# Opening of a hybrid encoder block re-ordered, and the w_up products kept in PSUM for the convolution

## The chip, the cores and the metric

The kernel runs on one core of a Trainium2 chip. A core has TensorE (matrix products, with weight loads that overlap them), VectorE, ScalarE, GpSimd, and SyncE, whose queue (SP) issues most of the DMAs; SBUF is the working memory, PSUM the eight banks into which TensorE writes. The metric is the device time of one execution in microseconds (us).

## The reference

One layer of a bidirectional encoder: 1024 positions, 1024 features, float32. A conditioning vector c gives six vectors of 1024 (shift, scale and gate, twice). The block is two token mixers in parallel, then a feed-forward network with a convolution over positions:

```python
ada = jax.nn.silu(c) @ w_ada[i] + b_ada[i]
shift1, scale1, gate1, shift2, scale2, gate2 = jnp.split(ada, 6, axis=-1)
h = rmsnorm(x, g_mix[i]) * (1 + scale1) + shift1
qa, ka, va, qb, kb, vb, ga, gb = jnp.split(h @ w_in[i], split_at, axis=-1)
oa = mixture_of_dilations(qa, ka, va, rel_bias)           # 8 heads of 64
ob = neighbourhood_attention_2d(qb, kb, vb, na_rpb[i])    # 8 heads of 64
merged = sigmoid(ga) * (oa @ w_branch_dil[i]) + sigmoid(gb) * (ob @ w_branch_na[i])
x = x + gate1 * (merged @ w_out[i])
h2 = rmsnorm(x, g_ffn[i]) * (1 + scale2) + shift2
u = depthwise_conv_seq(h2 @ w_up[i], conv_w[i], conv_b[i])   # width 3, centred
u_val, u_gate = jnp.split(u, 2, axis=-1)                     # 2816 each
x = x + gate2 * ((gelu(u_gate) * u_val) @ w_down[i])
return rmsnorm(x, g_final)
```

w_ada has 6144 columns, w_in 5120, w_up 5632.

## The kernel before

Features lie on the 128 partitions, positions on the free axis in two halves of 512. x comes transposed, as eight tiles of 128 features. Every large product is done in three passes: each operand is split into a rounded high part and a low remainder, and high x high, high x low and low x high are summed in PSUM. So every operand needs a ScalarE copy (the high part, `whi`, `h`, lines 57 and 207) and a subtraction on VectorE or GpSimd (the low part, lines 61 and 209).

**Opening** (from line 384, its order on all engines written out by hand). SP loads x's first half, then w_ada's first quarter, parts of w_in's q, k and v columns, further quarters of w_ada, and x's second half. In the meantime TensorE multiplies the identity with itself (`warm`, line 215), a product that nothing reads. ScalarE squares x (line 185), VectorE adds the squares in two groups of four, TensorE sums them over features with one-column products against ones (`add_sums`, line 98). `rstd_of` gives the root mean square, `bcast` spreads it by four transposes into a PSUM bank (`pb`). Of `ada`'s first 2048 values (shift1, scale1) only a quarter is needed at a time: a quarter is eight rows of w_ada, times c. VectorE sums six rows (`ada_rows`), TensorE takes the other two and that sum by one-column products (`ada_sums`, line 153).

Then come four pieces, q = 0 to 3. Each finishes a quarter of `ada` (`piece_bias`, lines 274 and 276), makes two feature tiles of h (`modulate`: VectorE multiplies x by scale and `pb`, ScalarE adds the shift and rounds, VectorE takes the low part), and lets TensorE add these two tiles into two 512-column products (q and k of the first heads, `qk_products`, lines 84 to 86) and into four groups of 256 columns (v, lines 246 to 248). Between these stand the next quarter's rows and sums. Afterwards come the other v half, the statistics of x's second half (`square_sums`, `bcast`), the writing out of q and k, and h's second half.

**Middle.** Attention heads, then the branch products, the gates and w_out. There x is read a second time from HBM.

**w_up** (from about 840 us). It has 22 blocks; each is a two by two block product done with seven products of combined operands instead of eight. `STEPS` names them: 11 x B11, S2 x T2, S1 x T1, S3 x T3, 12 x B21, S4 x B22, 22 x T4, each of 12 matmuls of 512 columns, into four PSUM banks a, b, c and d (`pj`, a ring of six). `products` (line 1191) adds the banks together on VectorE: line 1217 after the second step, 1219 after the third, 1222 after the fourth, 1230 after the sixth, 1234 after the seventh. `a_operands` prepares the weights (GpSimd lines 1159 to 1161 and 61, ScalarE line 57). The results go to the convolution: `conv_in` (line 1425) on ScalarE for the middle tap, `conv_taps` (line 1431) on VectorE for the other two, in six pieces. For the first three blocks the convolution waits until both halves of a row block are there. In the two remaining banks lie the statistics (`pcol`, `pbc`), and later the staging copies for w_down (`moved`).

Outside the hand-ordered parts a planner orders each engine's instructions when the program is built: it runs through them with estimated durations and takes by priority what its estimates find ready. It also gives out the buffers. So another cost or place in one part can move instructions in a later one.

Of the kernel before, what the change touches and what calls it, by code (L numbers as in the profile page):

```python
# [29 lines left out]
def hybrid_encoder(tc, xT, c, w_ada, small, w_in, p1_bias, p23_bias, na_bias, ln2_mult, ident, w_br, w_out,  # L30
# [83 lines left out]
    def h_tile(dtype=FR):  # L114
# [8 lines left out]
    homes = iter([(qkpool, "kl", 4)] + [(qkpool, n, b) for n, b in (("qs", 4), ("ks", 4), ("qb", 2))  # L123
                                        for _ in range((3, 3, 1)[("qs", "ks", "qb").index(n)])]
                 + [(early, "wada", 3)] * 2 + [(adapool, "wada", 4)] * 4 + [(qkpool, "qb", 2), (early, "wada", 3)])
# [19 lines left out]

    def ada_sums(parts, pa=None, stop=True, n=4, new=None):
# [15 lines left out]
    def ada_rows(wt, ts, acc=None):  # L162

        for t in ts:
            if acc is None:
                acc = wt[t]
                dve.tensor_scalar(acc, acc, cs[:, t:t + 1], None, OP.mult)
            else:
                dve.scalar_tensor_tensor(acc, wt[t], cs[:, t:t + 1], acc, OP.mult, OP.add)

    def x_load(hf, ks=range(KT)):
        x = []
        for k in ks:
            x.append(h_tile(FT))
            sp.dma_start(x[-1], xT[k][:, halves[hf]])
        return x
# [22 lines left out]
    def modulate(x, hf, ks, pb):  # L199

        last = ()
        for k in [*ks, None]:
# [7 lines left out]
            last = k is not None and (lo, t, b, f(hi))  # L210

# [57 lines left out]
    act.activation(sig, cs, AF.Sigmoid)  # L269
    dve.tensor_tensor(cs, cs, sig, OP.mult)  # L270
# [113 lines left out]
    with tc.manual_schedule(engines={e.engine for e in (sp, act, dve, pool, pe)}):  # L384
# [11 lines left out]
        wt.append(ada_load(3))  # L396
        x.append(x_load(1))
        qk_w = [[wpool.tile([128, KT, 128], FR, name=n) for n in ("whi", "wlo")] for _ in range(2)]
# [3 lines left out]
        first = ps_s.tile([128, 512], FT, name="pv", bufs=3)  # L402
        stage = [None, first]
# [12 lines left out]
        warm(12, first[:, :128], True)  # L416
        stage[0] = ps_n.tile([128, 512], FT, name="pcol")
        qk_split(0, (pool, pool))
        v_split(v_raw, (pool, pool), slice(0, 4), v_w[0])
        pvs = [v_banks()]  # L420
        for q in range(4):
            ks = range(2 * q, 2 * q + 2)
            if q == 2:
                v_raw1 = v_load(0, 1)
            piece_bias(q, pa)
            modulate(x[0], 0, ks, pb)
            qk_products(ks)
            if q < 3:
                ada_rows(wt[q + 1], range(6))
            if q == 0:  # L430
                qk_split(1, (dve, dve))
                v_split(v_raw, (dve, dve), slice(4, 8), v_w[0])
            if q == 2:
                v_split(v_raw1, (dve, dve), slice(0, KT), v_w[1])
            if q == 3:
                accs = sq_accs()
                square(x[1], accs, range(8), dve)
            v_products(0, (0, 1), ks)
            if q < 3:
                pa = ada_sums([(wt[q + 1][t], cs[:, t:t + 1]) for t in (6, 7)], stop=False)  # L440
                ada_sums([(wt[q + 1][0], ones)], pa)
# [1334 lines left out]
```

## Time and profile before

| | us |
|---|---|
| median of 3 runs | 1524.02 (1523.12 to 1525.61) |
| the profiled execution | 1522.23 |
| its span in the profile | 1520.5 |
| TensorE busy in the span | 1484.7 |
| mean granted TensorE clock | 0.991 |

A group's row in the profile reads: line, engine, operation, what is written from what, form, count, then busy us and mean ns, then the idle time before and what ended it. A timeline row reads: start, duration, engine, line, operation, operands. A row of waits: engine and line, what it waited for, total us, times, longest. A row of windows: start and end, length, then for PE, PEld (weight loads), DVE (VectorE), ACT (ScalarE) and POOL (GpSimd) busy us and count; then the granted clock, the busy share of the DMA engines, and GB/s. Matmuls are pipelined, so the duration of one (0.39 us) is longer than the distance to the next (0.23 us), and PE can count as busy though it waited for a moment.

### The profile page before, as it was taken

The page shows a single profiled execution, that of the slowest core. Times are in us where ns is not written, and L with a number is a line of the kernel's source. Part 1 is how long each engine was busy: PE and PEld are TensorE (multiplying, and loading weights), DVE is VectorE, ACT ScalarE, POOL GpSimd, SP SyncE. Part 2 cuts the span into 40 slices and gives each one's busy share as a digit, 9 for nine tenths or more (in the row PEclk, how much of TensorE's full clock was granted, in tenths as well). Part 3 has the DMA queues.
Part 4 walks back from the last instruction along what each step waited for, and adds up shares of the span by engine and source line. Part 5 has one row for each costly group of instructions (what it writes and reads, how often), then busy time and mean ns, then how long its engine had stood idle before and what let it go on. Part 6 is the DMA issues. An engine that isn't in the chain of part 4 may idle for free.

```text
span 1520.5 us, 21650 instructions
## 1 busy us (share of the span) xinstructions
PE 1484.7 (98%) x7680; PEld 1263.0 (83%) x7680; DVE 964.0 (63%) x1768; ACT 770.2 (51%) x1439; POOL 751.7 (49%) x624
## 2 busy tenths in 40 slices
PE   8999999999999999999999989999999998999997
PEld 8888888889798998878888868888888887878787
DVE  5775345465545655645515898766666668787765
ACT  4331566665655666643346553444444447575542
POOL 1021343424234454522268588776666665778721
PEclk9999999999999999999999999999999999999999
DMA  9567332434645555577644122222222224513323
GB/s 354 191 239 258 100 109 75 147 87 136 182 134 151 143 159 164 171 253 234 199 155 139 70 84 83 101 101 84 83 82 83 83 78 153 199 58 130 113 56 111
DMA packets 117299, 210.27 MB, mean 138 GB/s; under 512 B 42788, under 2 KB 55716, under 8 KB 117156
## 3 DMA queue, kind: packets, MB, share of 16 engines
q1 hardware_dynamic: 116920, 208.64, 42.6%
q8 instruction: 60, 0.98, 0.3%
q14 instruction: 47, 0.39, 0.1%
q10 hardware_dynamic: 272, 0.26, 0.1%
HBM read 163.58 MB, written 42.66 MB: 136 GB/s over the span
## 4 chain that ended last, share of the span: by engine, by line
PE 77%; DMA 6%; DVE 6%; POOL 5%; ACT 3%; issue 2%; SPq 0%; DVEq 0%; POOLq 0%; ACTq 0%
PE pj L84 10%; PE pj L86 10%; PE pj L85 10%; PE pj L1209 10%; PE pj L1210 10%; PE pj L1211 10%; PE pj L367 3%; PE O L937 2%; DMA wraw<-w_down 1%; POOL wsl L61 1%; DVE big L1431 1%; PE T L924 1%; PE S L902 1%; DMA fb<-fcs 1%; PE O L768 1%
## 5 line engine op out<-in xcount | busy, mean ns | idle before, releaser
L61 POOL TENSOR_TENSOR wlo<-wraw,whi 128x512 fp32r<-128x512 f32 (+1 forms) x94 | 116.1, 1257 | 172.0 <-ACT whi L57 138.0
L84 PE MATMUL pj<-h,whi 128*128 128x512 f32 x448 | 184.7, 412 | 2.2 <-ACT h L207 2.2
L85 PE MATMUL pj<-h,whi 128*128 128x512 f32 x448 | 176.1, 393 | 2.1 <-DVE h L209 2.1
L86 PE MATMUL pj<-h,wlo 128*128 128x512 f32 x448 | 175.9, 393 | 0.0
L61 POOL TENSOR_TENSOR wsl<-big,wsh 128x512 fp32r<-128x512 f32 (+1 forms) x86 | 116.7, 1379 | 45.0 <-ACT wsh L57 44.2
L641 POOL TENSOR_TENSOR wlo<-wraw,whi 128x512 fp32r<-128x512 f32 x58 | 75.1, 1306 | 116.2 <-ACT whi L640 103.5
L591 DVE TENSOR_TENSOR tl<-T,th 128x512 fp32r<-128x512 f32 (+3 forms) x120 | 77.2, 654 | 87.2 <-ACT th L590 85.8
L583 ACT ACTIVATE P<-P,st 128x256 f32<-128x256 f32 x128 | 64.2, 502 | 94.3 <-DVE st L582 94.3
L1431 DVE SCALAR_TENSOR_TENSOR big<-wc,sm,big 128x256 f32<-128x256 f32 (+1 forms) x129 | 100.8, 826 | 15.1 <-ACT big L1425 15.1
L86 PEld LDWEIGHTS pj<-h,wlo 128*128 128x128 f32 x448 | 84.1, 188 | 18.5
L85 PEld LDWEIGHTS pj<-h,whi 128*128 128x128 f32 x448 | 84.7, 189 | 13.9 <-DVE h L209 3.4
L84 PEld LDWEIGHTS pj<-h,whi 128*128 128x128 f32 x448 | 84.5, 189 | 14.1 <-ACT h L207 2.8
L57 ACT ACTIVATE whi<-wraw 128x1024 fp32r<-128x1024 f32 (+2 forms) x51 | 49.4, 971 | 70.8 <-PE pj L85 26.0
L915 POOL TENSOR_SCALAR P<-P,stb 128x288 f32<-128x288 f32 (+1 forms) x32 | 40.1, 1254 | 88.3 <-DVE stb L912 72.7
L61 POOL TENSOR_TENSOR wsl<-wraw,wsh 128x384 fp32r<-128x384 f32 (+1 forms) x46 | 53.6, 1186 | 57.8 <-ACT wsh L57 57.7
L1431 DVE SCALAR_TENSOR_TENSOR big<-pj,sm,big 128x512 f32<-128x512 f32 (+1 forms) x129 | 66.4, 563 | 15.7 <-ACT big L1425 15.7
L590 ACT ACTIVATE th<-T 128x512 fp32r<-128x512 f32 (+3 forms) x120 | 65.5, 565 | 20.4 <-PE T L924 13.0
L57 ACT ACTIVATE wsh<-big 128x1024 fp32r<-128x1024 f32 (+1 forms) x43 | 42.9, 997 | 51.8 <-POOL big L1160 37.0
L549 POOL TENSOR_TENSOR vv<-vv 128x512 fp32r<-128x512 f32 (+1 forms) x40 | 41.9, 1066 | 47.0 <-ACT vv L548 45.8
L582 DVE CUSTOM_DVE_ANT_0 P<-S,bias 128x256 f32<-128x256 f32 x128 | 48.8, 419 | 22.2 <-POOL bias L679 11.5
L908 ACT ACTIVATE P<-P,stb 128x288 f32<-128x288 f32 (+1 forms) x64 | 36.4, 569 | 47.6 <-DVE stb L906 47.6
L1457 ACT ACTIVATE big<-big 128x1024 f32<-128x1024 f32 x22 | 23.3, 1061 | 65.3 <-DVE big L1431 65.3
(426 smaller groups left out, 4744.0 us busy)
## 6 DMA issues: line engine op xcount, KB each, us to landing
wraw<-w_in SPq DMA_DIRECT2D x34, 512.0 KB
wada<-w_ada SPq DMA_DIRECT2D x31, 512.0 KB
big<-w_up SPq DMA_DIRECT2D x22, 512.0 KB
wraw<-w_up SPq DMA_DIRECT2D x22, 512.0 KB
as<-big SPq DMA_DIRECT2D x22, 512.0 KB
big<-as SPq DMA_DIRECT2D x22, 512.0 KB
wraw<-w_down SPq DMA_DIRECT2D x24, 384.0 KB
gs<-gs SPq DMA_DIRECT2D x32, 256.0 KB
```

What stands on the lines that cost most here:

```text
L57: act.activation(hi, raw, AF.Copy)
L61: lo_eng.tensor_tensor(lo[:, i:i + step], raw[:, i:i + step], f(hi)[:, i:i + step], OP.subtract)
L84: pe.matmul(psum, whi[:, k0 + k], mhi, start=k == 0, stop=False)
L85: pe.matmul(psum, whi[:, k0 + k], mlo, start=False, stop=False)
L86: pe.matmul(psum, wlo[:, k0 + k], mhi, start=False, stop=k == n - 1)
L590: act.activation(th[:m, :n], pt[:m, :n], AF.Copy)
L591: dve.tensor_tensor(tl[:m, :n], pt[:m, :n], f(th)[:m, :n], OP.subtract)
L641: pool.tensor_tensor(lo[:, i:i + n], raw[:, i:i + n], f(hi)[:, i:i + n], OP.subtract)
L1209: pe.matmul(psum, whi[:, k], bhi, start=j < 4 and k == 0, stop=False, skip_group_check=True)
L1210: pe.matmul(psum, whi[:, k], blo, start=False, stop=False, skip_group_check=True)
L1211: pe.matmul(psum, wlo[:, k], bhi, start=False, stop=k == n - 1, skip_group_check=True)
L1431: dve.scalar_tensor_tensor(y[:, dst], src, wt, y[:, dst], OP.mult, OP.add)
```

## The change

In the opening: c and the identity are loaded by ScalarE's queue. x's layout in HBM is changed, and its first half comes in four DMAs of two tiles each. TensorE sums the last two squared tiles itself. It takes w_ada's rows 0 and 1 directly; VectorE's sum of rows lies in a PSUM bank. Of the identity passes 9 + 2 + 2 + 2 + 2 + 5 are left, standing between the sums. x is multiplied by `pb` ahead of the pieces (four tiles by VectorE, four by GpSimd from a copy), and `scaled` then makes the high part in one ScalarE pass and, in a second pass, the float32 value from which VectorE takes the low part. The products of a tile ask for the low part last. Rows of w_ada are summed ahead, seven by VectorE and one by TensorE in two of the quarters. GpSimd takes more low parts. The last quarter of w_ada goes to other buffers, and w_in's second v half is loaded early. Among the v groups behind the pieces, the sums and the broadcast of x's second half are moved.

In w_up: for all blocks but the last, the result of the fourth step is written to a PSUM bank of the tags `pcol` and `pbc` in turn, and that of the seventh stays in its own bank.

```diff
-    sp.dma_start(idt, ident)
-    sp.dma_start(cs, c)
+    act.dma_start(cs, c)
+    act.dma_start(idt, ident)
...
+    def ada_rows_load(j):
+        rows = [h_tile(FT) for _ in range(KT)]
+        for t, w in enumerate(rows):
+            sp.dma_start(w, w_ada[j][:, t])
+        return rows
...
+    def ada_rows(wt, acc, ts, first, last):
         for t in ts:
+            col, dst = cs[:, t:t + 1], wt[t] if t == last else acc
+            if t == first:
+                dve.tensor_scalar(dst, wt[t], col, None, OP.mult)
             else:
+                dve.scalar_tensor_tensor(dst, wt[t], col, acc, OP.mult, OP.add)
...
+    def scaled(x, k):
+        hi, lo = h[0, k] = h_tile(), h_tile()
+        t, b, g = stage[k % 2], ada[:, k:k + 1], am1[:, k:k + 1]
+        act.activation(hi, x, AF.Identity, bias=b, scale=g)
+        act.activation(t, x, AF.Identity, bias=b, scale=g)
+        return lambda: dve.tensor_tensor(lo, t, f(hi), OP.subtract)
...
     def qk_products(ks):
         for k in ks:
-            for p, w in zip(qk_psum, qk_w):
-                product(p, w, lambda k: h[0, k], ks=[k])
+            mhi, mlo = h[0, k]
+            for x_, (part, m) in enumerate(((0, mhi), (1, mhi), (0, mlo))):
+                for p, w in zip(qk_psum, qk_w):
+                    pe.matmul(p, w[part][:, k], m, start=k + x_ == 0, stop=k == KT - 1 and x_ == 2)
...
-        warm(28, first[:, :128], True)
+        warm(9, idle, True)
         accs = sq_accs()
-        square(x[0], accs, range(8), dve)
-        pcol = square_sums(accs, lambda: warm(8, first[:, :128], True))
-        ada_rows(wt[0], range(3))
+        square(x[0], accs, range(6), dve)
+        last = [early.tile([128, 512], FT, name="mt", bufs=3) for _ in range(2)]
+        for sq, xk in zip(last, x[0][6:]):
+            act.activation(sq, xk, AF.Square)
+        pcol = ps_n.tile([128, KT], FT, name="pcol")
+        for i, sq in enumerate(accs + last):
+            add_sums(pcol, sq, i == 0, i == 3)
+            if i == 0:
+                warm(2, idle, True)
+            if i == 1:
+                warm(2, idle, True)
+            if i == 2:
+                pa = ada_sums([(wt[0][0], cs[:, 0:1])], stop=False)
+                warm(2, idle, True)
+        ada_rows(wt[0], acc, range(2, 6), 2, 7)
         rs = rstd_of(pcol, 4)
-        warm(4, first[:, :128], True)
+        qk_split(0, (pool, pool))
+        ada_sums([(wt[0][1], cs[:, 1:2])], pa, stop=False)
         pb = bcast(rs, ps_n, "pbc")
-        ada_rows(wt[0], range(3, 6), wt[0][0])
-        pa = ada_sums([(wt[0][t], cs[:, t:t + 1]) for t in (6, 7)], stop=False)
-        ada_sums([(wt[0][0], ones)], pa)
-        warm(12, first[:, :128], True)
+        pbs = early.tile([128, 512], FT, name="mt", bufs=3)
+        act.activation(pbs, pb, AF.Copy)
+        ada_rows(wt[0], acc, range(6, 8), 2, 7)
+        for k in range(2):
+            dve.tensor_tensor(x[0][k], x[0][k], pb, OP.mult)
+        warm(2, idle, True)
+        ada_sums([(wt[0][7], ones)], pa)
+        warm(5, idle, True)
         for q in range(4):
             ks = range(2 * q, 2 * q + 2)
             piece_bias(q, pa)
-            modulate(x[0], 0, ks, pb)
+            if q == 0:
+                for k in range(2, 4):
+                    dve.tensor_tensor(x[0][k], x[0][k], pb, OP.mult)
+                stage = [ps_n.tile([128, 512], FT, name=n) for n in ("pcol", "pbc")]
+            low = [scaled(x[0][k], k) for k in ks]
+            if q == 0:
+                v_split(v_raw, (pool, pool), slice(0, 4), v_w[0])
+                for k in range(4, 8):
+                    pool.tensor_tensor(x[0][k], x[0][k], pbs, OP.mult)
+            if q == 1:
+                qk_split(1, (pool, pool))
+                v_split(v_raw, (pool, pool), slice(4, 8), v_w[0])
...
+            if q == 0:
+                pa = ada_sums([(wt[1][t], cs[:, t:t + 1]) for t in (6, 7)], stop=False)
+                v_parts(0, range(4), ks, (0,))
+                ada_sums([(wt[1][5], ones)], pa)
+                v_parts(0, range(4), ks, (1, 2))
+                continue
...
-        pcol = square_sums(accs)
-        v_products(1, (1,), range(8))
-        pb = bcast(rstd_of(pcol, 4), ps_n, "pbc")
+        pcol = square_sums(accs, lambda: v_products(1, (1,), range(8)))
+        rs = rstd_of(pcol, 4)
+        v_products(1, (2,), range(8))
+        pb = bcast(rs, ps_n, "pbc")
...
             elif j == 3:
-                dst = p["b"] if in_psum else c["v"]
+                dst = p["b"] if in_psum else spare() if spare else c["v"]
...
-                dst = psum if in_psum else c["t"]
+                dst = psum if in_psum or spare else c["t"]
...
+                            spare=None if t == FF - 1 else
+                            lambda: ps.tile([128, 512], FT, name="stage", tag=next(stages)))
...
-        "xT": x[0][_POS].T.reshape(KT, 128, S),
+        "xT": x[0][_POS].T.reshape(4, 2, 128, 2, 512).transpose(3, 0, 2, 1, 4),
```

More of the change, by code (lines that the diff above doesn't have):

```diff
@@ L401, in hybrid_encoder @@
         qk_psum = [ps_g.tile([128, 512], FT, name="pj") for _ in range(2)]
[L402 to L409 removed]
+        acc = ps_s.tile([128, 512], FT, name="pv", bufs=3)
+        pvs = [v_banks()]
+        idle = pvs[0][0][:, :128]
@@ L1189, in a_operands, with products @@
         yield
-    def products(st, n, moving, done, seq=range(7), in_psum=False, hold=None):
+    def products(st, n, moving, done, seq=range(7), in_psum=False, hold=None, spare=None):
         p, c = {}, {}
```

88 lines of the change are left out of this document (50 added, 38 removed).

## The prediction

> **What bounds the kernel now.** I read the page first (engines, slices, clock), then busy time by stage, then the two stages where TensorE is not full.
>
> ```profile
> PE 1484.7 (98%) x7680; PEld 1263.0 (83%) x7680; DVE 964.0 (63%) x1768; ACT 770.2 (51%) x1439; POOL 751.7 (49%) x624
> PE 77%; DMA 6%; DVE 6%; POOL 5%; ACT 3%; issue 2%; SPq 0%; DVEq 0%; POOLq 0%; ACTq 0%
> ```
>
> TensorE carries the kernel. A gain must either take work off TensorE's path or close a stretch in which it waits or runs at half clock. The stages (start:end, time, then busy us per engine in the order PE, PEld, DVE, ACT, POOL, then the granted clock):
>
> ```profile
> 0.00:26.00 26.00, 23.06 (x149) 22.82 (x149) 10.98 (x19) 11.23 (x17) 5.16 (x8) 0.87 0.91 331
> 26.00:63.00 37.00, 32.66 (x221) 28.95 (x220) 32.64 (x51) 13.52 (x23) 0.00 (x0) 1.00 0.80 301
> 840.00:930.00 90.00, 82.33 (x356) 66.09 (x356) 83.44 (x104) 43.83 (x62) 63.47 (x41) 0.96 0.20 70
> 930.00:1262.00 332.00, 332.00 (x1465) 274.61 (x1465) 229.18 (x336) 147.05 (x180) 231.46 (x176) 1.00 0.26 92
> ```
>
> The steady w_up loop (930 to 1262) has no hole: 332.0 us for 1465 matmuls, 0.227 us each. VectorE has a third of its time free there, so cheaper VectorE work is worth nothing in that stretch. The change can pay in the opening (0 to 63) and at the start of w_up (840 to 930), where VectorE is busy 83.4 of 90 us.
>
> **The opening as it is.** Timeline rows (start, duration, engine, line, what):
>
> ```profile
> 2.71 9.42 PE L215 MATMUL pv<-idt 128*128 128x128 f32 x56 [2.71 <-DMA idt<-ident]
> ...
> 14.64 0.95 PE L98 MATMUL pcol<-ones,sq 128*128 128x1 f32 x8
> ...
> 16.43 0.60 PE L111 MATMUL pbc<-idt,rs 128*128 128x128 f32 x4
> 19.08 1.85 PE L153 MATMUL pada<-ones,kl 128*128 128x1 f32 x8
> 20.78 5.35 PE L215 MATMUL pv<-idt 128*128 128x128 f32 x24
> 22.42 0.76 DVE L206 SCALAR_TENSOR_TENSOR pcol<-h,am,pbc 128x512 f32<-128x512 f32 x1
> 23.21 0.69 ACT L207 ACTIVATE h<-pcol,ada 128x512 fp32r<-128x512 f32 x1 [2.67 <-DVE pcol L206]
> 25.89 0.48 PE L84 MATMUL pj<-h,whi 128*128 128x512 f32 x1
> 27.64 0.50 PE L85 MATMUL pj<-h,whi 128*128 128x512 f32 x1 [1.27 <-DVE h L209]
> 59.85 0.28 PE L246 MATMUL pv<-vwh,h 128*128 128x256 f32 x1
> 62.72 0.28 PE L246 MATMUL pv<-vwh,h 128*128 128x256 f32 x1
> ```
>
> The sums of squares end at 15.6 and the first h product starts at 25.89. The tile h was there at 23.9: in between TensorE was finishing 24 identity passes. Windows of one us give the reason (PE, PEld, DVE, ACT, POOL, clock, DMA share, GB/s):
>
> ```profile
> 5.00:6.00 1.00, 1.00 (x6) 1.00 (x6) 0.15 (x1) 0.63 (x1) 0.00 (x0) 1.00 0.86 186
> 9.00:10.00 1.00, 1.00 (x12) 1.00 (x11) 0.85 (x2) 0.91 (x3) 0.00 (x0) 1.00 1.04 389
> 18.00:19.00 1.00, 1.00 (x11) 1.00 (x11) 0.46 (x1) 0.96 (x2) 0.37 (x1) 1.00 1.00 385
> 19.00:20.00 1.00, 1.00 (x7) 1.00 (x7) 0.00 (x0) 0.94 (x3) 1.00 (x2) 0.53 1.02 397
> 39.00:40.00 1.00, 1.00 (x6) 0.79 (x6) 0.96 (x2) 0.00 (x0) 0.00 (x0) 1.00 1.05 387
> ```
>
> Identities run at 6 per us until about 9 and at 12 after, though the column says 1.00 throughout: the array starts at half speed, and some 6 us of unbroken identities released it. Then, after two us of one-column sums during which PE is "busy" without a hole, the grant falls at 19 and the sums slow from 0.95 to 1.85 us for eight. So one-column sums do not hold the clock.
>
> **The change in the opening, part by part.** *Chain to the first product.* Removed ahead of it: 28+8+4+12 identities (two passes each). Put in: 9, then 2 after each of the first three groups of sums, 2 and 5 later. Two more groups of eight for the squares (four now, as the last two tiles are summed by TensorE) and eight each for w_ada's rows 0 and 1. Nine identities last 18 x 0.168 = 3.0 us (9.42/56), half of what released the clock before, so I take half clock up to the products. The first sum needs four tiles squared and added; x now has SP's queue to itself from the start and comes in 512 KB pieces. At 387 GB/s (the later loads of 2 KB rows, 39:40) I get 6.3 us for it, at the early 186 GB/s 9.2; I take 7.5. From there: four groups of sums and row 0, 5 x 1.85 = 9.25; three pairs of identities, 12 x 0.168 = 2.0: the sums of squares end at 18.8 (before: 15.6). Row 1 1.85; four transposes 2 x 0.60; two identities 0.7; the summed rows 1.85; five identities 1.7: TensorE is free at 26.0. The tile h needs the sums at 24.3, two small VectorE steps (0.5) and 0.7 on ScalarE: 25.5. **First product 26.0 against 25.89: no gain**, though the chain looks shorter. At full clock throughout it would be about 18.5: the squares end at 7.5 + 5 x 0.95 + 12/12 = 13.3, and then VectorE's last two w_ada rows, their sums and the 1.2 us to h set it.
>
> *The four pieces.* TensorE's work in one is 12 products of 0.227, 24 of 0.12 (59.85 to 62.72 are 24) and 24 sums of 0.117: 8.4 us, the last without sums 5.6. Before: 3 x 8.4 + 5.6 = 30.8 in 25.89 to 62.72 = 36.8, so 6.0 us of waiting (from TensorE's waits, 0 to 75):
>
> ```profile
> PE pj L84 <- ACT h L207: 2.2, 3, 1.1
> PE pj L85 <- DVE h L209: 2.1, 4, 1.3
> ```
>
> (the rest is hidden in the pipelined durations). Now x is scaled ahead, so the VectorE step of 0.76 before h goes; the low half is asked for after four products instead of one; two pieces have 16 sums instead of 24. New work 8.4 + 7.5 + 7.5 + 5.6 = 29.0. The low half now needs two ScalarE passes and one subtraction, 0.69 x 2 + 0.76 after the start, while four products last 0.9: I leave 0.4 of waiting a piece, 1.6, total 30.6. That is 6.2 less. The products begin at half clock. In the w_up stage (rows below) the clock came back after 4.86 us of dense matmuls; here the dense run starts with the summed rows' end at 24.3 (identities, then 5.4 us of slow products), so I put the release at 29.2, after 3.2 us of products at half speed: 1.6 lost. Net 4.6.
>
> *What pays for it.* x's multiplication by the broadcast moves: tiles 0 to 3 on VectorE before the first piece and 4 to 7 on GpSimd, with low halves of the weights beside them. These hide behind pieces 0 and 1 (15 us); without that cover GpSimd's four tiles would cost about 6.6 us (its row of 6.63 for four 512-column tiles stands below). The ScalarE queue takes c and ident (two issues ahead of its first square, which waits for x anyway). wt[3] is eight loads instead of four and w_in's second V half goes ahead of the seven w_ada pairs: a few issues on SP, whose stores behind them have 15 us. After the pieces the broadcast of x's second half now stands behind a third V group.
>
> ```profile
> 71.88 0.76 DVE L206 SCALAR_TENSOR_TENSOR pcol<-h,am,pbc 128x512 f32<-128x512 f32 x1
> ...
> 76.61 0.23 PE pj L258
> ```
>
> h's second half started 4.7 us before TensorE asked; I count that start 2.7 us later (a V group is 24 x 0.12 = 2.9). A tile takes VectorE two steps of up to 0.76, TensorE six products, 1.36, so TensorE catches up: 0.8 us lost. Opening: -4.6 + 0.1 + 0.8 = **-3.7 us** (from -13 with a full clock to +3 with a late release).
>
> **w_up.** The sum of step 3 and the last sum stay in PSUM, so for 21 of 22 blocks the six taps of one half read PSUM (as pj does now) instead of SBUF (wc):
>
> ```profile
> L1431 DVE SCALAR_TENSOR_TENSOR big<-wc,sm,big 128x256 f32<-128x256 f32 (+2 forms) x12 | 13.7, 1158 | 0.0
> L1431 DVE SCALAR_TENSOR_TENSOR big<-pj,sm,big 128x512 f32<-128x512 f32 (+2 forms) x12 | 6.3, 563 | 0.0
> ```
>
> These are the groups of 884.0 to 911.4, four taps of each length in either row: from SBUF 13.7 us, from PSUM 6.3. With all of them from PSUM VectorE is 7.4 us shorter there (in the steady loop its gain is worth nothing). These taps stand ahead of a sum that TensorE needs (two rows of TensorE's waits, two windows, two timeline rows):
>
> ```profile
> PE pj L1209 <- DVE wc L1219: 3.9, 1, 3.9
> PE pj L1209 <- ACT wsh L57: 2.4, 2, 1.3
> 907.00:910.00 3.00, 1.20 (x4) 0.67 (x4) 3.00 (x2) 1.54 (x2) 3.00 (x3) 0.99 0.00 0
> 910.00:917.00 7.00, 4.86 (x12) 3.85 (x13) 5.39 (x6) 2.51 (x3) 7.00 (x5) 0.52 0.30 119
> 911.41 0.68 DVE L1219 TENSOR_TENSOR wc<-pj,held 128x512 f32<-128x512 f32 x1
> 911.17 6.63 POOL L61 TENSOR_TENSOR wsl<-big,wsh 128x512 fp32r<-128x512 f32 x4
> ```
>
> L1219 would come some 7 us sooner, the wait of 3.9 goes, and with it the half clock that it set off: 4.86 us of matmuls at 0.5 cost 2.4. With 0.5 of the weight waits (GpSimd is beside the same taps), **-6.8** (from 0, if another wait takes the place, to -8.7, if the weight waits go whole). Late next is GpSimd's wsl: after L1219's twelve products I count 24 more before it, 36 x 0.227 = 8.2 us from 908.2, 916.4, and its first part is there at 911.17 + 6.63/4 = 912.8. At the end of w_up nothing changes: its last block keeps SBUF.
>
> **Sum**: 1522.2 (the profiled run; span 1520.5) - 3.7 - 6.8 = 1511.7, **1512**. That run stands 1.8 under the median 1524.0.
>
> **The rivals.** *The clock holds (0.12).* If one-column sums count as work, the half clock ends in the opening, the first product comes at 18.5 instead of 26.0 and the cold 1.6 goes: 9.1 us more, 1503. The row 18:19 to 19:20 speaks against it. The Trainium skill, "TensorE: Matmul & The Clock Gate", Part 1, says that a busy window of about 3.4 us releases the clock and an idle one takes it back; read with PE busy as the page of the profile shows it, that rule gives this rival's 1503 and not 1512. This trace agrees only where the array streams wide operands: it dropped the clock under a PE that showed no idle.
>
> *The clock comes late (0.13).* A gap between the last identities and the first product (h only 0.5 us early) breaks the run of dense work; the 24 sums of piece 0 then keep the clock low and the piece lasts 16.8 instead of 8.4 + 1.6: 6.8 more, 1518.5.
>
> *GpSimd takes VectorE's place (0.11).* The planner, which orders w_up's matmuls by its own costs, may put wsl's products first; then the wait and the half clock stay, and of 6.8 only 1 comes: 1517.5. Both of the last two together (0.08): 1524, no change.
>
> *The other sign: banks (0.12).* Each block now holds one of six pj banks until its taps are done.
>
> ```profile
> 1090.95 0.68 DVE L1234 TENSOR_TENSOR wc<-pj,wc 128x512 f32<-128x512 f32 x1
> 1092.33 2.84 DVE L1431 SCALAR_TENSOR_TENSOR big<-wc,sm,big 128x255 f32<-128x255 f32 x5
> 1096.01 0.39 PE L1209 MATMUL pj<-T3hi,wsh 128*128 128x512 f32 x1
> ```
>
> The taps end 3.6 us after that sum, ahead of the next block's fourth bank at 1096.0, and two other banks are free by then. If TensorE waited all the same, 19 blocks at 1 us would give 1531; it decides from 0.55 us a block (10.5/19).
>
> **How the numbers follow.** My forecast has 0.44. Under it, the first two and the third rival lie from 1503 to 1518.5 and hold 0.80 with it: range 1501 to 1521 with the unknown ends; the forecast's own is 1507 to 1516. Faster by over 0.2% (3 us, about the spread of the runs) 0.80, within 0.08, slower 0.12.
>
> **What would show it.** Right: half clock in the records of the opening (eight sums in 1.85 us), first product near 26, pieces of 7.5 to 8.5 us without waits over 0.5, fourth piece done near 58; no wait on L1219 near 908 and no clock dip there; PE full from 930 to the end of block 21. Wrong: a first product before 20; a piece of 16 us; waits of matmuls on taps; a wait on wsl in place of L1219's.

## The result, and the profile after

| | before | after |
|---|---|---|
| median of 9 runs, us | 1523.44 (1521.80 to 1525.61) | 1519.89 (1514.64 to 1522.31) |
| profiled execution, us | 1522.23 | 1520.89 |
| its span, us | 1520.5 | 1518.6 |

The ratio is 0.9971, with a 95% interval of 0.9957 to 0.9985: 4.4 us faster (2.3 to 6.6). The prediction's sum has 10.5 (3.7 in the opening, 6.8 in w_up). The runs of the changed kernel lie twice as far apart as those before, 7.7 us against 3.8.

Busy time by stage, profile after, columns as in the prediction:

```profile
0.00:26.00 26.00, 19.91 (x106) 19.80 (x107) 11.55 (x22) 11.59 (x19) 2.68 (x6) 0.75 0.95 360
26.00:63.00 37.00, 36.14 (x253) 32.53 (x252) 27.47 (x40) 19.68 (x33) 15.61 (x12) 0.99 0.78 293
840.00:930.00 90.00, 85.80 (x373) 69.64 (x372) 77.04 (x109) 46.88 (x65) 67.51 (x47) 0.96 0.21 74
930.00:1262.00 332.00, 332.00 (x1467) 275.07 (x1466) 208.37 (x336) 145.00 (x178) 226.76 (x175) 1.00 0.26 88
1300.00:1520.00 220.00, 205.22 (x1009) 171.06 (x1007) 148.10 (x236) 104.67 (x185) 129.03 (x127) 0.98 0.32 107
```

The stretch with the pieces (26 to 63) is full now, 36.1 of 37 us. The start of w_up has 85.8 us of TensorE work instead of 82.3, at the same clock of 0.96. The steady loop is as full as it was; VectorE has 208 us there instead of 229, and it buys nothing.

Where the time went is seen best by the *lead*: the start of the same matmul in the profile after, less its start in the profile before (minus is earlier). In us, at a few places:

| place (time before) | lead |
|---|---|
| first h product (25.9) | -0.8 |
| end of h's first half (76) | -6.1 |
| first w_ada sums of the next group (98) | -5.3 |
| last of them (149) | -4.7 |
| heads (646) | -4.4 |
| first branch products (666) | -2.6 |
| first w_up product (846) | -2.2 |
| last w_up product but one (1278) | -6.1 |
| last w_down product on B11h (1482) | -1.8 |

So the two gains are there, 5.3 and 3.9 us, and nearly as much goes back: 0.6 before 149, 1.8 among the heads (a stretch of 3.4 us at half clock at 648, which the profile before does not have), 4.3 in w_down. One trace can't say which of these belong to the change and which to this one execution. The opening's TensorE rows after (start, duration):

```profile
6.09 3.92 PE L234 MATMUL pv<-idt 128*128 128x128 f32 x18 [6.09 <-DMA idt<-ident]
9.85 0.95 PE L98 MATMUL pcol<-ones,sq 128*128 128x1 f32 x8
13.66 1.84 PE L158 MATMUL pada<-cs,kl 128*128 128x1 f32 x8
16.36 1.71 PE L98 MATMUL pcol<-ones,mt 128*128 128x1 f32 x8
17.93 1.85 PE L158 MATMUL pada<-cs,kl 128*128 128x1 f32 x8
25.08 1.20 PE L308 MATMUL pj<-h,whi 128*128 128x512 f32 x2
```

Eight one-column sums take 1.71 to 1.85 us from 13.66 on, the half clock that was forecast; the first two groups took 0.95, so the clock had been up for a moment. ident, the second load on ScalarE's queue beside x, landed only at 6.1 (before: 2.7). At the start of w_up TensorE's waits after are:

```profile
PE pj L1281 <- POOL wsl L61: 2.4, 1, 2.4
PE pj L1279 <- ACT wsh L57: 0.9, 1, 0.9
```

L1219's wait of 3.9 is gone; one of 2.4 on GpSimd's low half stands in its place (rows of GpSimd, and of TensorE):

```profile
892.44 1.26 POOL L61 TENSOR_TENSOR xb<-wraw,xb 128x512 fp32r<-128x512 f32 x1
893.66 2.50 POOL L61 TENSOR_TENSOR wsl<-xb,wsh 128x512 fp32r<-128x512 f32 x2
```

```profile
892.19 0.40 PE L1280 MATMUL pj<-T1lo,wsh 128*128 128x512 f32 x1
894.99 0.79 PE L1281 MATMUL pj<-T2hi,wsl 128*128 128x512 f32 x1 [2.40 <-POOL wsl L61]
895.58 0.63 PE L1279 MATMUL pj<-T2hi,wsh 128*128 128x512 f32 x1
```

After it the matmuls start 0.43 us apart for some 5 us, instead of 0.23: the half clock came with this wait as it had with the other.

### The profile page after: what moved, and what is told of

Same layout as the page of the kernel before. It is cut to its first block, busy times and chain, and to the rows that moved or that the text cites. A ratio compares the mean times of both kernels' runs of the same rounds, so it can differ in the third digit from the quotient of the medians.

```text
span 1518.6 us, 21544 instructions
## 1 busy us (share of the span) xinstructions
PE 1482.7 (98%) x7620; PEld 1259.1 (83%) x7620; DVE 928.3 (61%) x1759; ACT 776.4 (51%) x1448; POOL 759.5 (50%) x634
## 4 chain that ended last, share of the span: by engine, by line
PE 70%; DMA 9%; POOL 7%; DVE 7%; issue 3%; ACT 3%; SPq 1%; DVEq 0%; POOLq 0%; ACTq 0%
PE pj L84 9%; PE pj L1281 9%; PE pj L86 9%; PE pj L1280 9%; PE pj L85 9%; PE pj L1279 9%; PE pj L397 2%; POOL wsl L61 2%; DMA wada<-w_ada 2%; DMA wraw<-w_down 2%; PE O L1007 2%; DMA fb<-fcs 2%; PE T L994 1%; PE S L972 1%; POOL wlo L61 1%
## 5 line engine op out<-in xcount | busy, mean ns | idle before, releaser
L84 PE MATMUL pj<-h,whi 128*128 128x512 f32 x432 | 178.9, 414 | 0.0
L86 PE MATMUL pj<-h,wlo 128*128 128x512 f32 x432 | 170.3, 394 | 0.0
L85 PE MATMUL pj<-h,whi 128*128 128x512 f32 x432 | 170.1, 394 | 0.0
L61 POOL TENSOR_TENSOR wsl<-big,wsh 128x512 fp32r<-128x512 f32 (+1 forms) x86 | 112.6, 1332 | 46.7 <-ACT wsh L57 46.4
L1501 DVE SCALAR_TENSOR_TENSOR big<-pj,sm,big 128x512 f32<-128x512 f32 (+2 forms) x192 | 99.6, 563 | 18.8 <-ACT big L1495 17.9
L84 PEld LDWEIGHTS pj<-h,whi 128*128 128x128 f32 x432 | 82.1, 190 | 10.8
L85 PEld LDWEIGHTS pj<-h,whi 128*128 128x128 f32 x432 | 82.1, 190 | 10.1
L1495 ACT ACTIVATE big<-pj,sm 128x512 f32<-128x512 f32 x64 | 49.2, 772 | 55.8 <-DVE pj L1300 35.2
L1300 DVE TENSOR_TENSOR pj<-pj,wc 128x512 f32<-128x512 f32 x33 | 22.9, 694 | 67.7 <-PE pj L1281 67.7
L652 DVE CUSTOM_DVE_ANT_0 P<-S,bias 128x256 f32<-128x256 f32 x128 | 48.8, 419 | 21.8 <-PE S L764 17.0
```

The source lines that it names most:

```text
L61: lo_eng.tensor_tensor(lo[:, i:i + step], raw[:, i:i + step], f(hi)[:, i:i + step], OP.subtract)
L84: pe.matmul(psum, whi[:, k0 + k], mhi, start=k == 0, stop=False)
L85: pe.matmul(psum, whi[:, k0 + k], mlo, start=False, stop=False)
L86: pe.matmul(psum, wlo[:, k0 + k], mhi, start=False, stop=k == n - 1)
L1501: dve.scalar_tensor_tensor(y[:, dst], src, wt, y[:, dst], OP.mult, OP.add)
```

## The experiments

All ratios are against the kernel before, run beside each; in us, 0.1% is 1.5. "First product" and "lead at 98" say what the opening did in the one profiled execution. "w_up" is from the start of its first matmul to that of its last but one, "w_down" from there to its last product on B11h (after: 843.66, 1271.66, 1480.21). The products behind that take 28.4 us in eleven of the traces, and 29.9 to 31.5 in filler, held_s2_by_vector and opening_12, where the clock is at half for a while.

| kernel | ratio (95%) | range of runs, us | first product | lead at 98 | w_up | w_down |
|---|---|---|---|---|---|---|
| before | 1 | 3.8 | 25.9 | 0 | 432.0 | 204.2 |
| after | 0.9971 (0.9957-0.9985) | 7.7 | 25.1 | -5.3 | 428.0 | 208.6 |
| opening_only | 1.0007 (0.9994-1.0020) | 9.5 | 21.9 | -8.4 | 431.9 | 207.1 |
| w_up_only | 0.9972 (0.9960-0.9984) | 6.5 | 24.4 | +0.8 | 427.0 | 205.0 |
| dense_opening | 0.9961 (0.9945-0.9976) | 3.6 | 24.8 | -5.0 | 427.9 | 205.3 |
| filler | 1.0018 (1.0003-1.0032) | 11.1 | 26.7 | -2.4 | 434.7 | 206.8 |
| held_opening_only | 0.9946 (0.9932-0.9960) | 2.9 | 21.8 | -7.9 | 431.9 | 205.4 |
| held_opening | 0.9918 (0.9903-0.9933) | 3.2 | 21.6 | -8.1 | 428.0 | 204.7 |
| opening_12 | 0.9984 (0.9971-0.9997) | 9.8 | 31.6 | +0.3 | 431.8 | 202.9 |
| ident_first | 0.9971 (0.9958-0.9983) | 5.4 | 26.3 | -2.8 | 428.3 | 208.1 |
| more_identities | 0.9941 (0.9929-0.9953) | 3.6 | 24.1 | -4.3 | 428.3 | 205.2 |
| s_low_by_vector | 0.9954 (0.9941-0.9967) | 9.9 | 27.6 | -1.6 | 428.3 | 202.7 |
| held_s2_by_vector | 0.9887 (0.9873-0.9901) | 5.2 | 25.7 | -5.1 | 424.1 | 202.8 |
| before_s2_by_vector | 0.9988 (0.9972-1.0003) | 8.0 | 24.2 | -1.8 | 433.4 | 203.5 |

A profiled execution is one draw, and not a typical one: in eight of the thirteen kernels below the first it is the slowest or second slowest of its runs. So leads show what can happen, the ratios what it is worth. The ranges rest on 5 to 12 runs each and grow with their number; beside the later kernels the kernel before spread from 1518.5 to 1529.5.

**The two halves of the change, each alone.** The first theory (G): both gains are real and are partly given back further on, in w_down above all, because its weights are not tied to TensorE's progress. Rivals: a gain passes whole (P); only the moments of half clock count (C).

```diff
-                            seq, hold=held if t == 2 else None,
-                            spare=None if t == FF - 1 else
-                            lambda: ps.tile([128, 512], FT, name="stage", tag=next(stages)))
+                            seq, hold=held if t == 2 else None)
```

> The changed opening with w_up as before. Theory G (gains at both places are real, and part is given back further on): the fourth piece ends about 6 us ahead of the kernel before, some 4.3 remain when w_up starts, the wait on L1219's sum (3.9 us before) and the half clock behind it stay, and the end is 1.5 to 3.5 us earlier. Rival P (a gain at a place passes whole to the end, and the missing part was never gained): the end is as far ahead as TensorE is after the fourth piece, 5 to 6 us. Rival C (only the moments of half clock decide): the end moves with the number of half-clock stretches and not with the opening.

The second kernel takes only the `spare` lines of the change into the kernel before.

> The opening as before, w_up's two sums in PSUM. Theory G: the wait on L1219's sum goes, a wait on GpSimd's wsl of 2 to 3 us and a stretch at half clock of 6.8 us come in its place, TensorE is 3.5 to 4.5 us ahead of the kernel before at 930, and 1 to 2 of these are left at the end. Rival P: all of them are there at the end, 3.5 to 4.5 us. The prediction's own term, 6.8 us ahead at 930, would show if there were no such wait without the new opening.

w_up alone gives 4.3 us (0.9972), all that the whole change gives, and its place shows it: w_up is 427.0 us long instead of 432.0. The wait on wsl and a stretch at half clock (3.4 us long, 6.8 in the changed kernel) came as there, so the new opening has no part in them. The opening alone gives nothing: 1.0007, between 0.9 us faster and 3.0 slower, although its profiled run, the fastest of its 12 (1519.09; median 1524.58), is 8.4 us ahead at 98. Its opening was not that of the changed kernel, though not one line differs there (TensorE):

```profile
5.99 3.71 PE L234 MATMUL pv<-idt 128*128 128x128 f32 x18 [5.99 <-DMA idt<-ident]
13.03 1.03 PE L158 MATMUL pada<-cs,kl 128*128 128x1 f32 x8
18.18 1.71 PE L158 MATMUL pada<-ones,qs 128*128 128x1 f32 x8
21.88 1.08 PE L308 MATMUL pj<-h,whi 128*128 128x512 f32 x2
```

Here the clock came up at 9.0, stayed up until 15.9 and came back at 22.7; in the changed kernel it was up from 9.6 to 13.0 and came back at 26.6. That is 3.2 us at the first product, from nothing in the code. (Times of the clock and leads are counted here from the start of each span, as the profile shows them; the recorded texts below have some of them 0.1 to 0.4 us off.)

**A denser opening, and 5 us put in.** The first kernel also has the broadcast's transposes ahead of row 1's sums (not shown in the cut).

```diff
+    sp.dma_start(idt, ident)
     act.dma_start(cs, c)
-    act.dma_start(idt, ident)
...
-        warm(9, idle, True)
+        warm(24, idle, True)
...
-                warm(2, idle, True)
+            warm(4, idle, True)
```

> The changed kernel with ident first on SP's queue, 24 identities before the first sums instead of 9, and four instead of two after each group. If the array counts the share of wide operands in a window, groups of 0.95 us of sums with 0.67 us of identities (some 43%) hold full clock: no half clock from 13 to 27, squares summed at 15.5 to 16.5 (17.9 at present there), first product at 21.5 to 22.5 instead of 25.1, fourth piece done 3 to 5 us sooner. If such a share doesn't hold it, the identities are only added: first product 26 to 28. The order of w_down's matmuls is the changed kernel's. Theory G: of 4 us gained, 1 to 2 are left at the end; rival P: all 4.

The clock was up from 8.1 to 32.0, so sums with identities between them can hold it. But eight passes of identities between two groups took 1.0 us, not 0.67, and the first product came at 24.8, not at 22. It is 5.9 us faster than before all the same, and its runs lie within 3.6 us. In w_down it loses 1.0 us against the profile before, with the order of the changed kernel, which lost 4.3, and with a larger lead: against G.

```diff
+            if t == 12:
+                next(stages)
+                filler = ps.tile([128, 512], FT, name="stage", tag=next(stages))
+                warm(30, filler[:, :128], True)
```

> The changed kernel with 30 identities (60 passes of 1/12 us, 5.0 us at full clock) on TensorE ahead of block 12 of w_up, where it has no hole, all orders behind it the same. Rival P: 5.0 us slower than the changed kernel. Theory G: w_down's weights, which TensorE waits for there (5.7 us in all, 2.9 before), are not tied to TensorE's progress alone; with TensorE 5 us later these waits shrink by 2 to 3.5, and the end is only 1.5 to 3 us later.

w_up became 6.7 us longer than in the changed kernel (434.7 against 428.0: the passes take 0.11 us each, not 1/12), and the ratio is 0.47% above the changed kernel's, 7 us. Nothing was taken back: G falls, P holds for what is lost in w_up. And this opening, the changed kernel's again, ran at half clock to the end (first sums 1.71 us, first product at 26.7):

```profile
4.61 4.21 PE L234 MATMUL pv<-idt 128*128 128x128 f32 x18 [4.61 <-DMA idt<-ident]
8.61 1.71 PE L98 MATMUL pcol<-ones,sq 128*128 128x1 f32 x8
```

**Is it the clock's course in the opening?** The second theory (L): whether and when the clock is released in the opening is a matter of chance since the change, and this takes the opening's gain. The rival (W): w_ada's loads between 88 and 150 and w_down give back whatever the opening brings. Both kernels take ident first on SP's queue and 20 identities ahead of the first sums, three (then 2, 1, 2, 2) in place of two between the groups, and six ahead of the products, with the broadcast ahead of row 1's sums; one has w_up as before, the other as changed.

```diff
-        warm(9, idle, True)
+        warm(20, idle, True)
...
+            warm(3 if i < 3 else 2, idle, True)
+        pa = ada_sums([(wt[0][0], cs[:, 0:1])], stop=False)
+        warm(1, idle, True)
```

> The changed opening with the clock held (ident first on SP's queue, 20 identities before the first sums, three after each of the first three groups, then 2, 1, 2, 2 and 6), w_up as before. Three looks at the changed opening so far had three courses of the clock (released at 9.4, at 9.8 for 3.4 us only, or not before 30.7) and the end of h's first half 9.1, 6.1 and 3.0 us ahead. Theory L (this lottery is what takes the opening's gain): here the clock is released near 8 to 9.5 and held, first product at 21.5 to 23, 8 to 9 us ahead at 76, and the end is 3 to 5 us earlier than with the changed opening alone, 1519.5 to 1521.5. Rival W (w_ada's loads between 88 and 150 and w_down give back whatever the opening brings): at most 1.5 us earlier, 1523 to 1524.5.

> The changed kernel with the same held opening. Theory L: 2 to 4 us earlier than the changed kernel and 0.5 to 2 earlier than with the 24 identities, 1514 to 1516. The planner gives w_down another order of matmuls than in the changed kernel (the one that it had with the changed opening alone): if an order has a price of 2 to 3 us, this comes out at 1517 to 1519 instead, with the leads equal until 1300. Rival W: 1516 to 1519, no better than with 24 identities.

The opening alone now gives 8.2 us (0.9946), the whole 12.5 (0.9918), and the runs close up to 3 us. The two parts add up: 0.9946 x 0.9972 is 0.9918. L holds, and W falls as an account of the whole. But both kernels came out below the ranges that L gave them (1515.4 against 1519.5 to 1521.5, and 1511.3 against 1514 to 1516): the clock's course is worth more than L said, or is not all of the difference. held_opening's opening (TensorE):

```profile
2.64 7.47 PE L234 MATMUL pv<-idt 128*128 128x128 f32 x40 [2.64 <-DMA idt<-ident]
9.95 0.95 PE L98 MATMUL pcol<-ones,sq 128*128 128x1 f32 x8
19.32 0.95 PE L158 MATMUL pada<-ones,qs 128*128 128x1 f32 x8
21.57 0.73 PE L308 MATMUL pj<-h,whi 128*128 128x512 f32 x2
```

Every group takes 0.95 us. The price that I had put on held_opening's order of w_down did not show: 204.7 there, as long as before.

```diff
-        warm(5, idle, True)
+        warm(12, idle, True)
```

> The changed opening alone with 12 identities instead of 5 ahead of the first product: the only difference in the trace ahead of w_down are 7 identities (0.6 to 1.2 us in the opening, behind h's chain, and a longer dense run for the clock), but the planner gives w_down another order of matmuls. If the order of w_down is what costs the changed opening its gain: 2 to 3 us earlier, 1521 to 1522.5. If it is the clock in the opening: 0 to 1.5 earlier. If neither: 0 to 1 later.

On opening_only: 0.23% faster, with a worse opening in its profiled run (clock up only at 32.3, first product at 31.6) and a w_down of 202.9 instead of 207.1, of which 3.1 us went again in the products behind it. The median of 1520.0 lies below all that was expected, nearest to the range of the order's price; but the intervals of the two ratios overlap slightly, and alone it settles nothing.

**Which of the two: ident's queue, or the number of identities?** N says that the length of the dense run ahead of the sums decides, Q that ident lands too late. One kernel moves ident to SP's queue and leaves all else; the other leaves ident where the change has it and takes the held opening's identities.

> The changed kernel with ident first on SP's queue instead of second on ScalarE's, nothing else; every engine has the changed kernel's order. ident should land near 2.7 instead of 4.6 to 6.5, and the nine identities end near 7, before the first sums are ready (8 to 9). Theory N (the length of the run of wide operands ahead of the one-column sums decides whether the clock is released): still a matter of chance, the median within 2 us of the changed kernel (1517 to 1521) and runs spread over 5 us or more. Rival Q (ident's late landing is what breaks it): 1511 to 1515 and a spread of 3 to 4 us as with the held opening.

> The held opening with ident left on ScalarE's queue as in the changed kernel. Theory N: the 20 identities begin 2 to 4 us later and end near 12 to 13.5, the sums start 2 to 3 us later than in the held opening, but the clock is released and held: 1512.5 to 1515, spread 4 us at most. Rival Q: no better than the changed kernel, 1517 to 1521.

ident_first is the changed kernel again, 0.9971 to the last digit. Its rows:

```profile
2.67 3.72 PE L234 MATMUL pv<-idt 128*128 128x128 f32 x18 [2.67 <-DMA idt<-ident]
8.58 1.37 PE L98 MATMUL pcol<-ones,sq 128*128 128x1 f32 x8 [2.18 <-DVE sq L198]
10.80 1.71 PE L98 MATMUL pcol<-ones,sq 128*128 128x1 f32 x8
26.34 1.20 PE L308 MATMUL pj<-h,whi 128*128 128x512 f32 x2
```

more_identities, with ident at 6.1 as in the changed kernel, has full clock in the sums:

```profile
6.12 6.55 PE L234 MATMUL pv<-idt 128*128 128x128 f32 x40 [6.12 <-DMA idt<-ident]
12.51 0.95 PE L98 MATMUL pcol<-ones,sq 128*128 128x1 f32 x8
24.14 0.73 PE L308 MATMUL pj<-h,whi 128*128 128x512 f32 x2
```

It starts its sums 2.7 us later than the changed kernel and is 4.6 us faster (0.9941). So Q falls: nine identities with two between the sums are too few, wherever ident comes from. These kernels change the run ahead of the sums and the identities between them together, so the ratios don't part the two; the traces, in the last section, show that the first decides whether the clock comes up and the second whether it stays. The difference between ident's two places with 20 identities is 0.23% (0.9918 against 0.9941, intervals that overlap a little).

**What holds the start of w_up.** If GpSimd took VectorE's place there, as the prediction's third rival had it, work taken off GpSimd must free it.

```diff
-        pair(ws, ("S2", "S1"), *s_tiles())
+        pair(ws, ("S2", "S1"), *s_tiles(), s_eng)
...
-        prep.append(a_operands(raw.pop(1), 4, s_home, sts[1], dve, spot=extra))
+        prep.append(a_operands(raw.pop(1), 4, s_home, sts[1], dve, spot=extra, s_eng=dve))
```

> The changed kernel, with the low halves of block 1's S2 and S1 made by VectorE instead of GpSimd. Theory of the third rival (at the start of w_up GpSimd takes VectorE's place): the wait of 2.4 us on wsl goes, with it the half clock from 894 to 901, and TensorE is 3 to 5 us further ahead at 930; the end is 2 to 4 us earlier than with the changed kernel, less what another order of w_down costs. Rival: VectorE's two steps of 0.7 us stand ahead of a sum that TensorE needs, and the wait moves to it: no change at 930.

The wait stayed at 2.0 us and w_up at 428.3: the edit took the wrong block. The operands that GpSimd makes at 884 to 904 are block 2's; block 1's are made before. The 2.6 us that this kernel gained on the changed one (0.9954, intervals that overlap) lie, as far as its profile shows, in w_down (202.7). With block 2's, on the held opening:

```diff
                                 w_at=None if t == 1 else 0, spot=extra if t == 1 else None,
+                                 s_eng=dve if t == 1 else pool)
```

> The held opening with the low halves of block 2's S2 and S1 by VectorE (the earlier run took those of block 1, which are made ahead of this place). At the start of w_up TensorE waits 2.4 us for GpSimd's wsl of block 2's S2, then 6.8 us at half clock. Third rival's reason: the wait goes and with it the half clock, 2 to 4.5 us more ahead at 930 than with the held opening (10.4 there), end at 1507 to 1509.5. Against it: the two steps of 0.7 us on VectorE stand behind the taps, and TensorE waits for them as long: 1510.5 to 1512.

TensorE's waits in 840 to 930, and the same window's row:

```profile
PE pj L1278 <- DVE wsl L61: 1.0, 1, 1.0
PE pj L1276 <- ACT wsh L57: 0.9, 1, 0.9
```

```profile
840.00:930.00 90.00, 87.14 (x390) 70.84 (x389) 79.83 (x114) 47.80 (x66) 66.75 (x46) 1.00 0.23 76
```

The wait of 2.4 has become 1.0, the half clock is gone (1.00), w_up is 424.1 us long: 7.9 us shorter than before, where 4.0 came off with the change. At 0.9887, 17 us faster than before, it is the fastest kernel of the study. The same edit alone, on the kernel before:

> The kernel before, with nothing changed but the low halves of block 2's S2 and S1, which VectorE makes instead of GpSimd. If the taps from PSUM are what lets VectorE take this work (two limits, one behind the other): VectorE is full from 884 to 911 before, 2.2 us more on it make L1219's sum later, the wait of 3.9 us on it grows to 5 to 6 and the half clock stays: 0 to 3 us slower than the kernel before. If relieving GpSimd was the whole of the 4.5 us that it brought on top of the held opening, and the PSUM taps had no part in it: 3 to 5 us faster.

```profile
PE pj L1209 <- ACT wsh L57: 4.7, 2, 3.6
PE pj L1209 <- DVE wc L1219: 1.8, 1, 1.8
```

w_up is 1.4 us longer there, and the ratio of 0.9988 is no measurable change. The wait did not grow where it was expected: the one on L1219 fell to 1.8, and TensorE waited for wsh instead, because ScalarE ahead of that copy stood 5.39 us for VectorE's taps (0.49 in the kernel before):

```profile
903.36 1.28 ACT L1457 ACT_TABLE_LOAD   x1 [5.39 <-DVE big L1431]
```

So VectorE was the first limit and GpSimd the second right behind it: the taps from PSUM are what lets VectorE take GpSimd's work, and neither step alone gets all of it. This rests on w_up in one profiled execution of each kernel (1.4 us longer on the kernel before, 3.9 shorter on the held opening). By the runs alone the edit brings 1.8 us (4.3 faster to 0.5 slower) and 4.7 us, which do not differ clear of noise.

**What remains of w_down.** The planner's order differs there although no line of w_down was touched: six orders in the fourteen kernels. The changed kernel's order lasted 205.3 to 208.6 us in four profiled executions (mean 207.2), that of opening_only, held_opening and more_identities 204.7 to 207.1, the order before 204.2, the two shortest 202.7 to 203.5 in two executions each. TensorE's waits there, from 1300 to 1470, are longer where it is longer. After:

```profile
PE pj L1281 <- POOL wlo L61: 2.6, 2, 1.5
PE pj L1279 <- ACT whi L57: 1.6, 2, 0.9
PE pj L1279 <- ACT wc L1285: 1.3, 3, 0.5
```

held_s2_by_vector:

```profile
PE pj L1278 <- POOL wlo L61: 1.5, 1, 1.5
PE pj L1276 <- DVE wc L1286: 0.2, 1, 0.2
```

5.7 us in all after (with 0.2 more on VectorE), 2.9 before, 1.7 here. That the order costs the changed kernel some 3 us is read from these traces; no run fixed the order with all else equal, and within one order they differ by up to 3.3 us, so its size stays open.

## Why the prediction was wrong

**The step that failed: "Opening: -4.6 + 0.1 + 0.8 = -3.7 us", taken whole into "1522.2 (the profiled run; span 1520.5) - 3.7 - 6.8".** At the end the opening alone brought nothing: it measured 1.1 us slower (0.9 faster to 3.0 slower). At the place itself the size was about right. Of the changed opening as it stands there are four profiled executions (opening_only, after, filler, s_low_by_vector), which are 8.4, 5.3, 2.4 and 1.6 us ahead at 98, 4.4 in the mean. Two things were wrong with the term. "So I take half clock up to the products" assumed a single course where there are several: the clock was released at 9.0, at 9.6, and twice only at 30 to 32, with first products at 21.9, 25.1, 26.7 and 27.6. The prediction's bounds for the term (-13 to +3) had room for this; its sum did not. And what stands behind 98 was put at nothing. At 149 the four are 6.0, 4.7 and 0.9 us ahead and 1.0 behind, 2.6 ahead in the mean. The piece between 98 and 149 was costed as "a few issues on SP, whose stores behind them have 15 us". In opening_only the v store stood behind w_ada's loads and ScalarE could not empty a bank (SP's issues, ScalarE's row, TensorE's wait):

```profile
124.55 2.87 SPq L133 DMA_DIRECT2D wada<-w_ada  x3
128.38 0.33 SPq L285 DMA_DIRECT2D vbc<-vs  x1
```

```profile
133.38 0.60 ACT L284 ACTIVATE vs<-pv 128x512 f32<-128x512 f32 x1 [6.57 <-DMA vbc<-vs]
```

```profile
PE pv L277 <- ACT vs L284: 1.5, 1, 1.5
```

The store took 5 us from its issue until ScalarE went on. More is lost in w_down (207.1 us in opening_only, 204.2 before), which the prediction did not have as a term at all: it named the planner only for w_up. With the clock held (held_opening_only) the lead of 7.9 us at 98 was still 8.2 at 149, and the opening alone gave 8.2 us at the end. That is 9.3 us more than without, though the mean lead at 98 is only 3.5 us larger; the traces do not explain the whole of this difference, and it stays open.

**The clock's rule, half of it right.** The prediction asked whether one-column sums count as work and settled it from one row ("one-column sums do not hold the clock"). Rightly: sums at 1.71 us with PE busy 6.00 of 6.00 us are in every trace of the changed opening. But it took the release for a length ("4.86 us of dense matmuls", "3.0 us, half of what released the clock before"), and did not ask how it would vary. The Trainium skill, "TensorE: Matmul & The Clock Gate", Part 1, says that the window is free-running and the same kernel therefore warms up after different numbers of matmuls; the four traces agree, with nearly 6 us between the best and the worst first product. Before the change 28 identities ran from 2.7 to 12.1, longer than two of the windows of 3.4 us in the last section, so one window was full of them at any phase; nine do not reach that.

**The w_up term: -6.8 forecast, -4.0 in the stage and -4.3 at the end.** "The wait of 3.9 goes" held. "And with it the half clock that it set off" did not. "Late next is GpSimd's wsl ... 916.4, and its first part is there ... 912.8" had the right engine and the wrong product: the planner put ten matmuls of block 2's S2 x T2 ahead of the twelve of S3 x T3, behind which they stood before, and there, at 892.6, its wsl, made from 893.7 on, is late. That is the third rival, priced at 5.8 us of loss and measured at 2.8 (4.0 instead of 6.8); the prediction had named a wait on wsl in place of L1219's as a sign against itself. That the full term was there to be had is shown by held_s2_by_vector: 7.9.

**What held.** Eight sums in 1.71 to 1.85 us; the fourth piece done at 56.7 (58); 0.8 lost at h's second half (6.1 to 5.3); the steady loop with no hole and no wait on banks; the end of w_up unchanged. The banks of the other-sign rival showed nowhere. That the first product came at 25.1, near the forecast's 26.0, is in part luck: the prediction's 0.168 us for an identity pass is a mean over both clocks (at half clock 18 passes take 4.0 us in filler, 0.22 each), its 1.85 us for eight sums is 1.57 to 1.71 from start to start, and the clock was up from 9.6 to 13.0. The rival "the clock holds" was not right: its condition, that one-column sums count as work, failed. Identities can hold the clock, and then the whole gives 12.5 us (held_opening), near the forecast's 10.5; but that is another kernel, and two misses offset each other there (8.2 for 3.7 in the opening, 4.3 for 6.8 in w_up).

## What to carry to other kernels

Work that only keeps TensorE's clock up is part of the critical path's timing: when it is cut, ask what the clock does in the worst phase, not in the profiled run, and read the spread of the runs beside the median. It is a hint and no proof: the standard deviation is 2.0 to 3.3 us in the six kernels with nine identities ahead of the sums and 1.1 to 2.1 in the five with 20 or 24, but 1.0 to 2.7 in the kernel before, from batch to batch. A gain counts at the end only after every later stage that a planner re-orders has been looked at again; compare the length of each stage, not only of those that were edited. When a wait is removed, the next one stands on another engine a few us later; moving a little of that engine's work to the one just freed was worth about as much again here (4.7 us by the ratios) as the edit itself (4.3).

## What the runs showed of the hardware

The granted clock in these traces changes only in stretches of 3.4 us and multiples (3.4, 6.8, 10.2, 13.7 and 20.5 us at half or full clock), at an offset that differs from run to run. The Trainium skill, "TensorE: Matmul & The Clock Gate", Part 1, gives 3413 ns for its window, and this agrees. It also says that an idle window takes the clock back; here it went back in windows in which PE shows no idle time, only one-column sums (after, 14 to 20):

```profile
14.00:20.00 6.00, 6.00 (x30) 6.00 (x30) 2.78 (x6) 1.25 (x3) 0.89 (x1) 0.50 1.01 373
```

Two or three identities of 128 columns between groups of eight sums were the difference. With three it held through the sums in three of four traces, and was lost at 16.5 in the fourth (held_s2_by_vector), so that margin is thin.

What decides can be worked out from the starts of TensorE's rows. Lay windows of 3.41 us forwards and back from the first change of the clock, and take the share of each that operands of 128 columns or more fill. In the first 44 us of all fourteen traces the clock came up behind windows with 86% or more (nine identities: 89% in opening_only, 100% in after, 90% in ident_first), and not behind those with 80% or less (the nine identities reach 65% of a window at most in filler, 62% in opening_12). It was lost behind windows with 42% or less (39% in after, 37% in held_s2_by_vector) and kept at 43% or more (44% in held_opening). Nine identities take 4.0 us at half clock (filler), so by an estimate from these numbers they fill 86% of some window in about half of the phases: 4.0 + 3.4 - 2 x 2.9 = 1.6 of 3.4 us. It was three of the six traces that have them.

The clock column can't be trusted at the start. Ahead of the first record of a change it shows full speed, though the sums there take 1.71 us. filler, 14 to 20:

```profile
14.00:20.00 6.00, 6.00 (x30) 6.00 (x30) 0.93 (x3) 0.06 (x1) 0.00 (x0) 1.00 1.01 369
```

The same 30 passes as in the row above it, at a nominal 1.00 and 0.50: read the clock from the number of passes.

A load of 64 KB that was the first on SP's queue landed at 2.7 us; as the second on ScalarE's queue, beside x on SP's, it landed between 4.6 and 6.5.
